# Decoder layer on one core: the last steps of the token-major projections tile by tile, and the output projection's operands in other memory, loaded and split earlier

## The chip, the core and the metric

One Trainium2 chip, one core. The time is that of one execution in device microseconds; the kernel is run several times, and the median is what counts.

## The reference

A decoder layer over 2048 tokens of width 1024, in float32. `_mixer` projects x, sends one part through a gated DeltaNet and the other through a chunked spatial gate, and projects both back; the residual and a layer norm follow. `_hierarchical_moe` then picks two of 64 experts for each token and applies them; a second residual and norm end the layer.

```python
def _mixer(h, w_in, ..., w_out):
    proj = h @ w_in
    qkv, z, b_raw, a_raw, u, v = jnp.split(proj, splits, axis=-1)
    y_dn = _gated_deltanet(qkv, z, b_raw, a_raw, ...)
    y_sgu = _spatial_gating(u, v, ...)
    return jnp.concatenate([y_dn, y_sgu], axis=-1) @ w_out
...
x = _layernorm(ALPHA * x + mixer(x))
x = _layernorm(ALPHA * x + moe(x))
```

## The kernel before

Every large product is made of three matmuls (`mm3`, L135 to L137): each operand is split into a high and a low part, high by ScalarE (`split`, L129), low by VectorE (L130), and high x high, high x low and low x high are summed in PSUM. The splits of one stream of pieces are handled by a `Feed` (from L188): `load` issues the transfers on the SyncE queue, up to two pieces ahead; `split` splits one piece; `get` hands out the oldest.

**Mixer.** Four chunks of 512 tokens, one after the other. Each begins with two token-major projections (`tokmajor`, L381): v and the gates' raw inputs, then v's second part. Four PSUM tiles of 128 tokens (`pz`) run through the eight pieces of the inner dimension (k); then `fin` evacuates the four tiles by the gelu (L439 and L442). Twenty channel-major projections (`chmajor`, tiles `pm`) follow. PSUM has four buffers for all of them, so a projection's first matmul waits until a buffer of the one ahead has been evacuated. Between those matmuls stand the steps of the chunk ahead, as generators that a small scheduler (`Threads`, L71) places: each `yield pe, lat` states how long the step keeps TensorE and how long its result will take, in estimated ns; while the main stream emits its matmuls, the side stream of the highest rank whose time has come is stepped. `attn` and `scan` (L750 to L800) are the DeltaNet's steps: `pa`, then for each of four tiles `pp`, `R`, `pv`, `V`, `pS`, `S`, `p4`, `sq`; `gate_norm` (L503) is the statistics (L509, L510) and the normalisation (L519) of the gelu's result.

**Output projection.** `main_c` works through units of chunk and tiles: three chunks of four tiles, then tiles 0 and 1, tile 2 and tile 3 of the last chunk. A unit has two halves of 512 output columns (z). y^T comes back from memory through a Feed (`yh`, `yl`); the weights `wo`, already split, come through `wload` and `wget`, in pairs of k, two pairs ahead, in a ring of three buffers. In unit KEPT (the third) the weights' ring is closed, and all eight pairs are loaded into a pool of their own (`o_k`), where the last units find them. VectorE evacuates a half with the residual (`xr`, L933). `norm`, `logits` and `route` of a unit run as side streams in the next. The four tiles `po2` use the same four PSUM buffers.

The pools are a stack: what is opened first lies lowest. `o_c` (constants), `o_y` (yh, yl), `o_w` (y^T as loaded), `o_b`, `o_s` and `o_v` (wo) lie over the mixer's pools, so the first use of a place waits for the last reader of what lay there.

**Experts.** 64 experts' weights (`er`) stream through a ring of tiles; the first of its loads are issued in the third unit and behind it (`loads`, L909).

Of the kernel before, what the change touches and what calls it, by code (L numbers as in the profile page):

```python
# [121 lines left out]
class K:  # L122
# [28 lines left out]
    def mixer(self, base, keep, moe_load):  # L151
# [42 lines left out]
        class Feed:  # L194
# [3 lines left out]
            def __init__(f, wp, pieces, parts, depth=2, ahead=2, width=WP):  # L198
# [2 lines left out]
                f.next_load = f.next_split = f.next_get = 0  # L201
                f.limit = len(f.src)

            def load(f):
                while f.next_load < len(f.src) and f.next_load < f.next_split + f.depth:
                    ap, n, width, dst = f.src[f.next_load]
                    r = f.wp.tile([P, f.width], F32, tag="raw", bufs=f.depth, name="wr")
                    rv = r[:, :n * width].rearrange("p (k n) -> p k n", k=n)
                    nc.sync.dma_start(rv, ap)
                    f.raw.append(rv)  # L210
                    f.next_load += 1

            def split(f):
                ap, n, width, dst = f.src[f.next_split]
# [157 lines left out]
        def xsl(t, k, s):  # L372
            return t[k // 2][:, k % 2, s]


        def xpiece(o, q):
            while len(o.xh) <= q:
                h, l = o.feed.get()
                o.xh.append(h), o.xl.append(l)

        def tokmajor(o, width, fin):  # L381

            ps = [psb.tile([P, 512], F32, tag="big", name="pz") for _ in range(TPC)]
            for k in range(KD):
                xpiece(o, k // 2)
                if k % 4 == 0:
                    hi, lo = o.feed.get()
                for t in range(TPC):
                    ts = slice(t * P, (t + 1) * P)
                    self.mm3(ps[t][:, :width], xsl(o.xh, k, ts), xsl(o.xl, k, ts), hi[:, k % 4, :], lo[:, k % 4, :],  # L390
                             k == 0, k == KD - 1)
                    yield 3 * width * 0.42
            for t in range(TPC):
                fin(t, ps[t])

        def chmajor(o, m, fin, last=False):
            if m in PART:
# [455 lines left out]
        scat = []  # L853
        plan = self.plan_consts(keep, cp2)

        def ytile(kp, n):
            return lambda: (yp.tile([P, 2, CH], FR, tag="yh", name="yh").rearrange("p a (b n) -> p (a b) n", n=n),
                            yp.tile([P, 2, CH], FR, tag="yl", name="yl").rearrange("p a (b n) -> p (a b) n", n=n))

        units = [(c, 0, TPC) for c in range(NCH - 1)] + [(NCH - 1, 0, 2), (NCH - 1, 2, 1), (NCH - 1, 3, 1)]
        KEPT = NCH - 2
        pcs = []
        for c, t0, nt in units:
            kp = 1024 // (nt * P)
            pcs += [(self.scr["yT"][c, :, k:k + kp, t0 * P:(t0 + nt) * P], kp, nt * P, ytile(kp, nt * P)) for k in range(0, KD, kp)]
        feed = Feed(wp2, pcs, 0, ahead=0, width=1024)
        wq, kept = [], {}

        def wload():
            if not todo:
                return
            u, z, k = todo.pop(0)
            q = [wpool.tile([P, 2, 512], FR, tag=f"w{j}{'' if u < KEPT else (z, k)}", bufs=3 if u < KEPT else 1, name=f"wo{j}") for j in range(2)]
            for j in range(2):
                nc.sync.dma_start(q[j].bitcast(F32), self.scr["w"][j][:, k:k + 2, z * 512:(z + 1) * 512])
            if u == KEPT:
                kept[z, k] = q
            wq.append(q)  # L880

        todo = [(u, z, k) for u in range(KEPT + 1) for z in range(2) for k in range(0, KD, 2)]

        def wget():
            q = wq.pop(0)
            if todo and (todo[0][0] < KEPT or kept):
                wload()
            return q
# [5 lines left out]
        def main_c(o, side):  # L894
            c, t0, nt = o.unit
            kp = 1024 // (nt * P)
            o.xr, o.ln, o.done, yy = [], 0, 0, []
            o.st = sp2.tile([P, TPC, 2, 6], F32, tag="st", name="st2")

            def residual(t):  # L900
                rows_of.append((o, t))
                if len(rows_of) > NXR:
                    v, z = rows_of[-1 - NXR]
                    run.until(lambda: v.done > z)
                tt = c * TPC + t0 + t
                o.xr.append(bp2.tile([P, D], F32, tag="xr", bufs=NXR, name="xr"))
                nc.sync.dma_start(o.xr[t], I["x"][tt * P:(tt + 1) * P, :])

            for z in range(2):  # L909
                ps = [psb.tile([P, 512], F32, tag="big", name="po2") for _ in range(nt)]  # L910
                for k in range(KD):
                    if z == 0 and k % kp == 0:
                        yy.append(feed.get())
                    if k % 2 == 0:
                        w = kept[z, k] if o.last else wget()
                    if z == 0 and k < min(nt, 2):
                        residual(k)
                    if z == 0 and k >= KD - 2:
                        for t in range(k - KD + 4, nt, 2):
                            residual(t)  # L920
                    for t in range(nt):
                        yh, yl = (v[:, k % kp, t * P:(t + 1) * P] for v in yy[k // kp])
                        self.mm3(ps[t], yh, yl, w[0][:, k % 2, :], w[1][:, k % 2, :], k == 0, k == KD - 1)
                        yield 650
# [6 lines left out]
                zz = slice(z * 512, (z + 1) * 512)  # L931
                for t in range(nt):
                    nc.vector.scalar_tensor_tensor(o.xr[t][:, zz], o.xr[t][:, zz], ALPHA, ps[t], OP.mult, OP.add)  # L933
# [49 lines left out]

        def route(o):
            c, t0, nt = o.unit
            lg = sp2.tile([P, TPC, 72], F32, tag="lg", name="lg")[:, :nt]
            nc.vector.tensor_tensor(lg, o.pl[:, :nt], bc(br.unsqueeze(1), [P, nt, 72]), OP.add)
            yield from self.route(c * TPC + t0, lg, sp2, psd, io64, rec, onesb, lts, eacc, scat)

        prev.sc = run.add(chain(attn(prev), scan(prev)), 0)  # L990
        before = None
        for _ in range(2):
            wload()
        feed.load()
        for _ in range(TPC + 1):
            run.step(prev.sc)
        for u, unit in enumerate(units):
            o = O()
            o.unit, o.before, o.last = unit, before, u > KEPT
            if u == KEPT:  # L1000
                run.finish(prev.sc)
                run.finish(*prev.outs)
                kst.close()
                right.close()
                moe_load()
                wpool = pool(kst, "o_k", 1, "right")
                for _ in range(2):
                    wload()
            run.main(main_c(o, run.add), 4)
            before = o  # L1010
        kst.close()
# [652 lines left out]
```

## Time and profile before

| what | us |
|---|---|
| median of three runs | 2387.25 |
| lowest and highest | 2384.0 and 2391.9 |
| the profiled execution | 2374.18 |
| its span | 2372.4 |
| TensorE busy | 2199.7 (93%) |
| VectorE busy | 1553.4 (65%) |
| ScalarE busy | 1074.5 (45%) |
| GpSimd busy | 535.4 (23%) |

All times of the profile are counted from the span's start. The profiled execution lies 13 us under the median. TensorE's busy time alone does not say where time is lost; for that the waits are read stage by stage: a wait is the idle time of an engine ahead of an instruction, put down to what ended last before it.

### The profile page before, as it was taken

The numbers are of one execution on the slowest core, as the hardware profiler recorded it, in microseconds if no ns is written. First come the engines' busy times: TensorE is split into PE (matmuls) and PEld (weight loads), VectorE is DVE, ScalarE is ACT, GpSimd is POOL, SyncE is SP. The second block draws the span as 40 slices with busy tenths as digits, with TensorE's granted clock in tenths as the row PEclk, the third lists the DMA queues.
The fourth block names the chain that finished last, engine by engine and source line by source line (L and its number), as shares of the span: only waits on it lengthen the run. The fifth ranks groups of instructions, "written<-read, shape, count | busy, mean of one in ns | idle before, by whom it ended". The sixth has DMA issues, their size and how long they took to land.

```text
span 2372.4 us, 32860 instructions
## 1 busy us (share of the span) xinstructions
PE 2199.7 (93%) x11146; PEld 1587.2 (67%) x11146; DVE 1553.4 (65%) x2543; ACT 1074.5 (45%) x1448; POOL 535.4 (23%) x549
## 2 busy tenths in 40 slices
PE   6999999999989989899499999999999999999966
PEld 5877877877787877788374584567457456745732
DVE  4775677677666756557683693577369357836959
ACT  2543254345425422212373583566258356635822
POOL 1113222221222221123521221122122111212115
PEclk8999999999999999999699999999999999999979
DMA  4333234233414356682599999999999999999946
GB/s 150 100 116 112 67 111 120 72 90 102 124 52 126 93 170 227 222 292 98 214 342 407 379 409 408 403 402 399 393 395 388 390 399 371 394 397 385 389 160 285
DMA packets 218898, 601.97 MB, mean 254 GB/s; under 512 B 49632, under 2 KB 70624, under 8 KB 216928
## 3 DMA queue, kind: packets, MB, share of 16 engines
q1 hardware_dynamic: 199840, 563.92, 64.5%
q0 software_dynamic: 18304, 33.77, 3.8%
q8 instruction: 90, 1.47, 0.3%
q10 hardware_dynamic: 576, 2.10, 0.2%
q14 instruction: 88, 0.72, 0.1%
HBM read 557.14 MB, written 65.60 MB: 262 GB/s over the span
## 4 chain that ended last, share of the span: by engine, by line
PE 54%; DMA 24%; DVE 10%; issue 4%; ACT 3%; another core or an unknown queue 2%; POOL 1%; SPq 1%; POOLq 0%; ACTq 0%; DVEq 0%
DMA er<-in_w_e 21%; PE pm L135 5%; PE pm L137 5%; PE pm L136 5%; PE pg L1384 3%; PE pu L1384 3%; PE po L135 2%; PE po L136 2%; PE po L137 2%; DVE elo L130 2%; PE epd L1426 2%; PE epd L1427 2%; PE epd L1429 2%; DMA y<-scr_y 1%
## 5 line engine op out<-in xcount | busy, mean ns | idle before, releaser
L130 DVE TENSOR_TENSOR elo<-er,ehi 128x1024 fp32r<-128x1024 f32 x468 | 549.6, 1219 | 146.8 <-ACT ehi L129 127.6
L129 ACT ACTIVATE ehi<-er 128x1024 fp32r<-128x1024 f32 x468 | 477.9, 1056 | 133.5 <-DMA er<-in_w_e 74.6
L135 PE MATMUL pm<-xh,whi 128*128 128x512 f32 x640 | 270.3, 422 | 5.6 <-ACT vg L442 5.6
L1437 POOL DMA_INDIRECT scr_y<-f,tix x54 | 78.2, 1449 | 865.8 <-DVE f L1436 700.8
L137 PE MATMUL pm<-xh,wlo 128*128 128x512 f32 x640 | 256.3, 400 | 0.0
L136 PE MATMUL pm<-xl,whi 128*128 128x512 f32 x640 | 256.1, 400 | 0.0
L130 DVE TENSOR_TENSOR wlo<-wr,whi 128x1024 fp32r<-128x1024 f32 (+1 forms) x104 | 134.8, 1296 | 70.9 <-ACT whi L129 70.9
L135 PEld LDWEIGHTS pm<-xh,whi 128*128 128x128 f32 x640 | 123.4, 193 | 30.6 <-ACT vg L442 6.1
L137 PEld LDWEIGHTS pm<-xh,wlo 128*128 128x128 f32 x640 | 122.9, 192 | 29.8 <-DVE wlo L130 1.0
L136 PEld LDWEIGHTS pm<-xl,whi 128*128 128x128 f32 x640 | 123.6, 193 | 23.2 <-issue 1.0
L1384 PE MATMUL pg<-er,exT 128*64 128x512 f32 x480 | 136.4, 609 | 1.6 <-DMA er<-in_w_e 1.6
L135 PE MATMUL pg<-ehi,exh 128*128 128x512 f32 x312 | 133.6, 428 | 4.4 <-ACT ehi L129 2.6
L136 PE MATMUL pg<-elo,exh 128*128 128x512 f32 x312 | 127.8, 409 | 8.2 <-DVE elo L130 6.5
L130 DVE TENSOR_TENSOR exl<-ept,exh 128x512 fp32r<-128x512 f32 x78 | 50.2, 683 | 130.0 <-ACT exh L129 129.8
L1384 PE MATMUL pu<-er,exT 128*64 128x512 f32 x480 | 131.1, 593 | 0.0
L129 ACT ACTIVATE whi<-wr 128x1024 fp32r<-128x1024 f32 (+1 forms) x104 | 110.5, 1063 | 43.7 <-DMA wr<-in_w_v 19.3
L1420 PE MATMUL epd<-er,hTw 128*64 128x512 f32 x480 | 125.4, 603 | 2.4 <-DMA er<-in_w_e 2.4
L1426 PE MATMUL epd<-ehi,hT 128*128 128x512 f32 x312 | 126.9, 407 | 0.7 <-ACT hT L129 0.7
L1427 PE MATMUL epd<-elo,hT 128*128 128x512 f32 x312 | 124.6, 399 | 0.5
L135 PE MATMUL po<-wo,yh 128*128 128x512 f32 x256 | 107.0, 418 | 17.8 <-DMA wo<-scr_w 6.9
L137 PE MATMUL pg<-ehi,exl 128*128 128x512 f32 x312 | 123.0, 394 | 0.0
L135 PE MATMUL pu<-ehi,exh 128*128 128x512 f32 x312 | 122.9, 394 | 0.0
(331 smaller groups left out, 4482.6 us busy)
## 6 DMA issues: line engine op xcount, KB each, us to landing
er<-in_w_e SPq DMA_DIRECT2D x768, 512.0 KB
wr<-in_w_q SPq DMA_DIRECT2D x80, 512.0 KB
wo<-scr_w SPq DMA_DIRECT2D x48, 512.0 KB
y<-scr_y SPq DMA_DIRECT2D x14, 1024.0 KB
wr<-in_w_v SPq DMA_DIRECT2D x16, 520.0 KB
wr<-in_xT SPq DMA_DIRECT2D x16, 512.0 KB
wr<-scr_yT SPq DMA_DIRECT2D x16, 512.0 KB
xr<-in_x SPq DMA_DIRECT2D x16, 512.0 KB
```

Source lines behind the costliest of these rows:

```text
L129: nc.scalar.activation(hi, src, AF.Copy)
L130: (engine or nc.vector).tensor_tensor(lo, src, hi.bitcast(F32), OP.subtract)
L135: nc.tensor.matmul(out, xh, wh, start=start, stop=False)
L136: nc.tensor.matmul(out, xh, wl, start=False, stop=False)
L137: nc.tensor.matmul(out, xl, wh, start=False, stop=stop)
L1384: nc.tensor.matmul(ps[r, :], g.xT[:, k, r], g.ws[s][k][:, z * DE:(z + 1) * DE], start=k == 0, stop=k == KD - 1)
L1420: nc.tensor.matmul(pd[r, :], g.hT[:, k, r], g.ws[s][KD + k][:, zz], start=k == 0, stop=k == 3)
L1426: nc.tensor.matmul(pd, g.hT[0][:, k, :], hi_[:, zz], start=k == 0, stop=False)
L1427: nc.tensor.matmul(pd, g.hT[0][:, k, :], lo_[:, zz], start=False, stop=False)
L1429: nc.tensor.matmul(pd, g.hT[1][:, k, :], hi_[:, zz], start=False, stop=k == 3)
L1437: ins = nc.gpsimd.indirect_dma_start(out=self.scr["y"], out_offset=ioff(g.idx[:, 2:3]), in_=g.f, in_offset=None, bounds_check=2 * S - 1, o ...
```

## The change

Six parts. `staggered` goes through all but the last two k for all tiles, and then takes each tile through the last two k by itself; `tokmajor` evacuates a tile where it ends, and so does `main_c`. The pools are opened in another order: `m_b` of the mixer ahead of `m_x` and `m_w`, and `o_b`, `o_s` ahead of `o_y`, `o_w`, `o_v`, so that these last lie where x^T and the projections' weights lay. The first two loads of y^T and of wo, and two splits, stand ahead of the constants. The five steps of `attn` and `scan` that ran ahead of the first unit are gone; `attn`'s last step now states a latency. In unit KEPT the first three pairs of weights go through the old ring, fetched ahead in the unit before, and the other five into `o_k`. In the units from KEPT on an expert load is issued at every other k, and `lg` has two buffers.

```diff
+        bp = pool(left, "m_b", 2, "left")
         xp = pool(left, "m_x", 4, "left")
         wp = pool(left, "m_w", 2, "left")
-        bp = pool(left, "m_b", 2, "left")
...
+        def staggered(nt):
+            for k in range(KD - 2):
+                for t in range(nt):
+                    yield k, t, t == 0, False
+            for t in range(nt):
+                for k in range(KD - 2, KD):
+                    yield k, t, t == 0, k == KD - 1
...
+            for k, t, first, end in staggered(TPC):
+                if first:
+                    xpiece(o, k // 2)
+                    if k % 4 == 0:
+                        hi, lo = o.feed.get()
...
+                if end:
+                    fin(t, ps[t])
+                yield 3 * width * 0.42
...
-                yield 870, 0
+                yield 870, 0 if t < TPC - 1 else 2500
...
         cp2 = pool(base, "o_c", 1, "left")
+        bp2 = pool(base, "o_b", 2, "left")
+        sp2 = pool(base, "o_s", 1, "left")
         yp = pool(base, "o_y", 4, "left")
         wp2 = pool(base, "o_w", 2, "left")
-        bp2 = pool(base, "o_b", 2, "left")
-        sp2 = pool(base, "o_s", 1, "left")
         kst = ExitStack()
-        wpool = pool(kst, "o_v", 1, "left")
+        wpool = [pool(kst, "o_v", 1, "left")]
...
+            if len(kept) < 3:
+                q = [wpool[0].tile([P, 2, 512], FR, tag=f"w{j}", bufs=3, name=f"wo{j}") for j in range(2)]
+            else:
+                q = [wpool[1].tile([P, 2, 512], FR, tag=f"w{j}{z}{k}", bufs=1, name=f"wo{j}") for j in range(2)]
...
+        for _ in range(2):
+            feed.load_one()
+            wload()
+        for _ in range(2):
+            feed.split()
         g1 = cp2.tile([P, D], F32, name="g1")
...
+                    if end:
+                        nc.vector.scalar_tensor_tensor(o.xr[t][:, zz], o.xr[t][:, zz], ALPHA, ps[t], OP.mult, OP.add)
+                    yield 650
+                    if t < nt - 1:
+                        continue
...
-                    if u >= KEPT and len(loads) > RING[1]:
+                    if u >= KEPT and k % 2 and len(loads) > RING[1]:
                         loads.pop(0)()
...
-        for _ in range(2):
-            wload()
-        feed.load()
-        for _ in range(TPC + 1):
-            run.step(prev.sc)
...
-                kst.close()
                 right.close()
                 moe_load()
-                wpool = pool(kst, "o_k", 1, "right")
-                for _ in range(2):
-                    wload()
+                wpool.append(pool(kst, "o_k", 1, "right"))
+                wload()
```

What the scheduler makes of it, at three places. First the SyncE queue (SP) at the end of the second unit and the start of the third; `wr<-scr_yT` are loads of y^T, `wo` the weights, each pair of k being two loads. Before:

```order
190 L877 DMA wo_8642<-scr_w_63 128x2x512
191 L877 DMA wo_8643<-scr_w_64 128x2x512
192 L209 DMA wr<-scr_yT 128x1024
193 L209 DMA wr<-scr_yT 128x4x256 x2
194 L877 DMA wo_8807<-scr_w_63 128x2x512
195 L877 DMA wo_8808<-scr_w_64 128x2x512
196 L877 DMA wo_8811<-scr_w_63 128x2x512
197 L877 DMA wo_8812<-scr_w_64 128x2x512
198 L877 DMA wo_8820<-scr_w_63 128x2x512
199 L877 DMA wo_8821<-scr_w_64 128x2x512
```

Now:

```order
189 L209 DMA wr<-scr_yT 128x1024
190 L868 DMA wo_8702<-scr_w_63 128x2x512
191 L868 DMA wo_8703<-scr_w_64 128x2x512
192 L209 DMA wr<-scr_yT 128x4x256
193 L868 DMA wo_8749<-scr_w_63 128x2x512
194 L868 DMA wo_8750<-scr_w_64 128x2x512
195 L209 DMA wr<-scr_yT 128x4x256
196 L868 DMA wo_8820<-scr_w_63 128x2x512
197 L868 DMA wo_8821<-scr_w_64 128x2x512
198 L868 DMA wo_8829<-scr_w_63 128x2x512
```

Before, all of the third unit's weights stood behind the two y^T loads of 4x256; now two of its pairs (8702 with 8703, 8749 with 8750) stand ahead of the second of them.

VectorE (DVE) at the second border of chunk 1, where the gelu's statistics meet the scan of the chunk ahead (`S`). Before, from the end of the fourth group of statistics:

```order
498 L510 BN_AGGR mv<-st 128x2
499 L512 TENSOR_SCALAR rs<-mv 128x4
500 L519 TENSOR_SCALAR vg<-vg,mv,rs 128x128 x4
501 L130 TENSOR_TENSOR wlo<-wr,whi 128x1024
502 L790 SCALAR_TENSOR_TENSOR S_158<-S_157,eg,pS 128x128 x4
503 L794 TENSOR_TENSOR o<-o,p_4392 128x512
504 L367 TENSOR_REDUCE ro<-sq 128x4
```

Now, from the end of the third group:

```order
483 L524 BN_AGGR mv<-st 128x2
484 L526 TENSOR_SCALAR rs<-mv 128x4
485 L804 SCALAR_TENSOR_TENSOR S_157<-S_158,eg,pS 128x128 x4
486 L808 TENSOR_TENSOR o<-o,p_4295 128x512
487 L371 TENSOR_REDUCE ro<-sq 128x4
488 L812 TENSOR_TENSOR ro<-ro,rq_3505 128x4
489 L813 TENSOR_SCALAR ro<-ro 128x4
490 L523 BN_STATS st<-vg 128x6
```

`S` stood behind four groups, a normalisation and a split; now it stands behind three groups, and the fourth group follows it.

ScalarE (ACT) at the start of the output projection: the first splits `yh` and the scan's `V` and `sq`. Before:

```order
495 L693 ACTIVATE Q_154<-pq 64x2x64 x2
496 L129 ACTIVATE yh<-wr 128x1024
497 L786 ACTIVATE V<-pv 128x512
498 L129 ACTIVATE yh<-wr 128x1024
499 L366 ACTIVATE sq<-o 128x512
500 L786 ACTIVATE V<-pv 128x512
501 L129 ACTIVATE yh<-wr 128x1024
502 L366 ACTIVATE sq<-o 128x512
```

Now:

```order
498 L707 ACTIVATE Q_154<-pq 64x2x64 x2
499 L129 ACTIVATE yh<-wr 128x1024 x2
500 L800 ACTIVATE V<-pv 128x512
501 L370 ACTIVATE sq<-o 128x512
502 L129 ACTIVATE yh<-wr 128x1024
503 L800 ACTIVATE V<-pv 128x512
504 L370 ACTIVATE sq<-o 128x512
505 L129 ACTIVATE yh<-wr 128x1024
506 L800 ACTIVATE V<-pv 128x512
507 L370 ACTIVATE sq<-o 128x512
508 L800 ACTIVATE V<-pv 128x512
```

Two splits stand ahead of the scan's first `V`; the third and the fourth each stand behind a `V` and an `sq`.

## Rows read from the trace of the kernel before

**Rows 1.** Windows of each stage: length, busy time of each engine, granted clock, DMA share, GB/s.

```profile
0.00:837.00 837.00, 777.99 (x4562) 652.42 (x4563) 572.99 (x1178) 354.68 (x591) 190.88 (x256) 0.96 0.34 102
837.00:1124.00 287.00, 262.53 (x1517) 220.92 (x1516) 169.01 (x386) 60.76 (x96) 66.07 (x75) 0.96 0.60 206
1140.00:1164.00 24.00, 1.52 (x9) 0.70 (x9) 15.12 (x80) 0.82 (x4) 13.34 (x20) 0.50 0.25 89
1168.00:2249.00 1081.00, 1065.63 (x4776) 660.04 (x4777) 695.77 (x720) 619.49 (x717) 212.14 (x154) 1.00 1.01 390
```

**Rows 2.** Waits of PE at chunk 1's two borders: us, times, longest.

```profile
PE pp L355 <- DVE S L790: 2.5, 1, 2.5
PE pm L135 <- ACT vg L442: 1.9, 1, 1.9
PE pz L135 <- ACT vg L439: 1.7, 1, 1.7
```

**Rows 3.** Timeline of DVE behind chunk 1's second border: start, length, line, operation.

```profile
255.91 0.29 DVE L509 BATCH_NORM_STATS2 st<-vg 128x6 f32<-128x128 f32 x1
...
257.63 0.17 DVE L512 TENSOR_SCALAR rs<-mv 128x4 f32<-128x4 f32 x1
...
267.26 1.11 DVE L790 SCALAR_TENSOR_TENSOR S<-S,eg,pS 128x128 f32<-128x128 f32 x4
```

**Rows 4.** Waits of PE from 850 to 1070, in the output projection.

```profile
PE po L135 <- DMA wo<-scr_w: 6.9, 1, 6.9
PE po L135 <- ACT yh L129: 4.9, 2, 4.6
PE po L135 <- DVE xr L933: 3.1, 2, 2.4
PE po L135 <- issue: 2.9, 1, 2.9
PE pp L355 <- DVE dec L755: 2.5, 1, 2.5
PE po L136 <- DMA wo<-scr_w: 1.6, 2, 1.3
PE po L137 <- DVE yl L130: 0.9, 2, 0.5
```

**Rows 5.** Windows around four waits: busy time of each engine, granted clock, DMA share.

```profile
251.00:256.00 5.00, 4.57 (x21) 4.30 (x22) 3.64 (x7) 2.15 (x6) 3.01 (x2) 0.66 0.13 29
862.00:870.00 8.00, 6.58 (x19) 5.09 (x20) 1.83 (x2) 1.32 (x2) 0.00 (x0) 0.57 0.55 163
998.00:1008.00 10.00, 5.74 (x17) 4.30 (x18) 9.16 (x29) 4.05 (x4) 2.49 (x2) 0.66 1.03 384
1061.00:1066.00 5.00, 3.40 (x15) 2.83 (x16) 4.93 (x10) 0.00 (x0) 0.00 (x0) 1.00 0.00 0
```

**Rows 6.** Timeline of the SP queue at the output projection's start.

```profile
853.12 11.81 SPq L209 DMA_DIRECT2D wr<-scr_yT  x3
```

**Rows 7.** Timelines of ACT and DVE at the first to the second unit.

```profile
932.22 1.06 ACT L129 ACTIVATE yh<-wr 128x1024 fp32r<-128x1024 f32 x1 [5.04 <-PE po L136]
...
933.31 1.23 DVE L130 TENSOR_TENSOR yl<-wr,yh 128x1024 fp32r<-128x1024 f32 x1 [4.69 <-ACT yh L129]
```

**Rows 8.** Timeline of the SP queue at the second to the third unit.

```profile
984.54 11.60 SPq L209 DMA_DIRECT2D wr<-scr_yT  x3
996.25 3.02 SPq L877 DMA_DIRECT2D wo<-scr_w  x6
```

**Rows 9.** Timelines of DVE and POOL behind the third unit's start.

```profile
995.67 2.47 DVE L933 SCALAR_TENSOR_TENSOR xr<-xr,po 128x512 f32<-128x512 f32 x4
...
1006.53 3.33 POOL L962 TENSOR_TENSOR xr<-xr,b 128x1024 f32<-128x1024 f32 x1 [3.75 <-DVE xr L961]
```

**Rows 10.** Timeline of PE in the second unit, first and last of 27 matmuls.

```profile
945.75 0.40 PE L135 MATMUL po<-wo,yh 128*128 128x512 f32 x1
...
951.84 0.39 PE L137 MATMUL po<-wo,yl 128*128 128x512 f32 x1
```

More of the change, by code (lines that the diff above doesn't have):

```diff
@@ L202, in __init__, with load_one @@
                 f.limit = len(f.src)
+            def load_one(f):
+                ap, n, width, dst = f.src[f.next_load]
+                r = f.wp.tile([P, f.width], F32, tag="raw", bufs=f.depth, name="wr")
+                rv = r[:, :n * width].rearrange("p (k n) -> p k n", k=n)
+                nc.sync.dma_start(rv, ap)
+                f.raw.append(rv)
+                f.next_load += 1
             def load(f):
                 while f.next_load < len(f.src) and f.next_load < f.next_split + f.depth:
[L206 to L211, printed above, removed]
+                    f.load_one()
             def split(f):
@@ L823, in mixer, with ytile, wload, wget @@
         cp2 = pool(base, "o_c", 1, "left")
+        bp2 = pool(base, "o_b", 2, "left")
+        sp2 = pool(base, "o_s", 1, "left")
         yp = pool(base, "o_y", 4, "left")
         wp2 = pool(base, "o_w", 2, "left")
-        bp2 = pool(base, "o_b", 2, "left")
-        sp2 = pool(base, "o_s", 1, "left")
         kst = ExitStack()
-        wpool = pool(kst, "o_v", 1, "left")
+        wpool = [pool(kst, "o_v", 1, "left")]
+        def ytile(kp, n):
+            return lambda: (yp.tile([P, 2, CH], FR, tag="yh", name="yh").rearrange("p a (b n) -> p (a b) n", n=n),
+                            yp.tile([P, 2, CH], FR, tag="yl", name="yl").rearrange("p a (b n) -> p (a b) n", n=n))
+        units = [(c, 0, TPC) for c in range(NCH - 1)] + [(NCH - 1, 0, 2), (NCH - 1, 2, 1), (NCH - 1, 3, 1)]
+        KEPT = NCH - 2
+        pcs = []
+        for c, t0, nt in units:
+            kp = 1024 // (nt * P)
+            pcs += [(self.scr["yT"][c, :, k:k + kp, t0 * P:(t0 + nt) * P], kp, nt * P, ytile(kp, nt * P)) for k in range(0, KD, kp)]
+        feed = Feed(wp2, pcs, 0, ahead=0, width=1024)
+        wq, kept = [], {}
+        def wload():
+            if not todo:
+                return
+            u, z, k = todo.pop(0)
+            if len(kept) < 3:
+                q = [wpool[0].tile([P, 2, 512], FR, tag=f"w{j}", bufs=3, name=f"wo{j}") for j in range(2)]
+            else:
+                q = [wpool[1].tile([P, 2, 512], FR, tag=f"w{j}{z}{k}", bufs=1, name=f"wo{j}") for j in range(2)]
+            for j in range(2):
+                nc.sync.dma_start(q[j].bitcast(F32), self.scr["w"][j][:, k:k + 2, z * 512:(z + 1) * 512])
+            if u == KEPT:
+                kept[z, k] = q
+            wq.append(q)
+        todo = [(u, z, k) for u in range(KEPT + 1) for z in range(2) for k in range(0, KD, 2)]
+        def wget():
+            q = wq.pop(0)
+            wload()
+            return q
+        for _ in range(2):
[3 more added lines that the diff above has]
+            feed.split()
         g1 = cp2.tile([P, D], F32, name="g1")
@@ L854, in mixer @@
         plan = self.plan_consts(keep, cp2)
[L856 to L886, printed above, removed]
-                wload()
-            return q
         NXR, rows_of = 6, []
@@ L910, in main_c @@
                 ps = [psb.tile([P, 512], F32, tag="big", name="po2") for _ in range(nt)]
[L911 to L924, printed above, removed]
+                zz = slice(z * 512, (z + 1) * 512)
+                for k, t, first, end in staggered(nt):
+                    if first:
+                        if z == 0 and k % kp == 0:
+                            yy.append(feed.get())
+                        if k % 2 == 0:
+                            w = kept[z, k] if o.last else wget()
+                        if z == 0 and k < min(nt, 2):
+                            residual(k)
+                        if z == 0 and k >= KD - 2:
+                            for v in range(k - KD + 4, nt, 2):
+                                residual(v)
+                    yh, yl = (v[:, k % kp, t * P:(t + 1) * P] for v in yy[k // kp])
+                    self.mm3(ps[t], yh, yl, w[0][:, k % 2, :], w[1][:, k % 2, :], k == 0, k == KD - 1)
+                    if end:
[3 more added lines that the diff above has]
+                        continue
                     if z == 1 and (k + 1) % kp == 0 and feed.next_split < len(pcs):
                         feed.split()
-                    if u >= KEPT and len(loads) > RING[1]:
+                    if u >= KEPT and k % 2 and len(loads) > RING[1]:
                         loads.pop(0)()
```

21 lines of the change are left out of this document (5 added, 16 removed).

## Prediction

> **What bounds the kernel now.** I read the windows by stage first, then the waits of the matmul engine, then the granted clock around each wait, and last what the transfer queue and the side engines did there. In the mixer's 837 us and the output projection's 287 us TensorE is busy 93% and 91% of the time and the DMA share is 0.34 and 0.60 [rows 1]: there the matmuls and the holes between them set the time. In the expert stage, 1081 us long, TensorE is busy 98.6% and the DMA share is 1.01 [rows 1]; no hole is left in it. The change touches only the first two stages, so all it can win is holes on TensorE, and the reduced clock that follows some of them.
>
> The mixer's holes that the change touches are at the two borders after the token-major projections of chunks 1 to 3. The listed waits stand for chunk 1: 1.7 us for the gelu of the first projection (L439), 1.9 us for that of the second (L442), 2.5 us for S (L790) [rows 2]. Chunks 2 and 3 repeat them within 0.2 us. S is late since DVE stands in one long row of normalisation work: the first BN_STATS of a group starts at 255.91, its rs at 257.63, four such groups stand ahead of S, which runs at 267.26 [rows 3].
>
> In the output projection the waits are 6.9 and 1.6 us for wo, 4.9 for yh, 3.1 for the evacuation of the residual (L933), 2.9 marked issue, 2.5 for dec, 0.9 for yl: 22.8 us [rows 4].
>
> After some of these holes the clock goes from 2.4 to 1.2 GHz for a while. The loss is (1 - granted clock) x window: 0.34 x 5 = 1.7 us at 251, and the mixer has five such stretches among its nine border waits; 0.43 x 8 = 3.4 us at 862, the same again at 934, and 0.34 x 10 = 3.4 us at 998 [rows 5]. Together 8.5 + 10.2 = 18.7 us.
>
> **The change part by part.**
>
> *First border of the mixer.* The last two k are done tile by tile, and each tile is evacuated as it ends. The next projection's first tile needs the first PSUM tile, whose gelu now starts three tiles (18 matmuls) earlier; 1.7 us is covered. Chunks 1 to 3 win 3 x 1.7 = 5.2. Chunk 0's stays: there the scalar engine stands before a split that waits for its load.
>
> *Second border.* 1.9 + 2.5 = 4.4 us go in each chunk, but new ones come. The DVE rows show that S now stands right behind the third group of statistics and that the fourth group lies between it and the R that the next scan step needs. A group takes 1.7 us [rows 3]. Following each matmul to its producer I get about 1.4 us (pp for S), 1.9 (pv for R) and 0.9, in all 4.2. Bounds: nothing, and three groups of 1.7, 5.1. I take 4.2, as the queue is full there. Net 0.2 x 3, nothing.
>
> *Clock in the mixer.* Where a wait of 3.8 to 4.4 is cut into pieces, some of the five stretches should go. I keep three of five: 2 x 1.7 = 3.4 won. Bounds: all gone, 8.5; or four more come, -6.8.
>
> *Start of the output projection.* Before, the first y^T load is issued at 853.12, behind the constants and four weight loads [rows 6], since its tile lay over ones used to the end of the mixer. Now its memory is x^T's and the projection weights', free after the last projection (837), and two splits stand ahead of the constants, so they wait only for the side engines, still busy with the merge of chunk 3. The yh wait (4.9), dec (2.5) and yl (0.9) are 8.3. New: a split is 1.06 us on the scalar engine and 1.23 on DVE [rows 7], and the third and fourth are issued when their k comes; the ACT rows show V and sq of the scan ahead of each. Laying these durations out in the new order I get 1.3 for the first piece, 1.85 for the third, 3.7 for the fourth, whose split stands behind an sq that itself waits for matmuls just ahead. Sum 6.9; bounds nothing and four full splits, 4 x 2.3 = 9.2. Clock: 3.4 now, I leave 1.7. Net 8.3 - 6.9 + 1.7 = 3.1.
>
> *Between the halves of a unit.* The 3.1 us of waits for L933 are two: 2.4, the longest, from the third to the fourth unit, and 0.7 at the border of the first unit's halves [rows 4]. The second goes: 0.7.
>
> *First to second unit.* The 2.9 us stand while yh (932.22), yl (933.31) and four evacuations end one after the other [rows 4, 7]. With the tiles evacuated as they end, nothing is left to wait for: 2.9 and the clock's 3.4, 6.3.
>
> *Second to third unit.* Six weight loads are issued at 996.25, behind three y^T loads that held the queue for 11.6 us from 984.54 [rows 8]; TensorE waits 6.9 and then 1.3 of the 1.6 [rows 4]. By the rows of the queue two pairs of these weights now stand ahead of that held load. 8.2 and the clock's 3.4 go: 11.6. What is late next is the norm: transposes of the first normalised tile stand 60 matmuls behind the border; 26 take 951.84 - 945.75 = 6.09 us, so 60 take 14.1 [rows 10]. From the evacuation to the end of the bias on POOL it is 1006.53 + 3.33 - 995.67 = 14.2 [rows 9], of which three evacuations (1.85) now lie ahead of the border, and the last, behind a split, may come up to 1.2 + 1.8 later. So 12.3 to 15.5 against 14.1: a wait of 0 to 1.4. I take 1.4. Net 10.2.
>
> *Third to fourth unit.* 2.4 + 0.3 go, 1.4 comes for the same reason: 1.3.
>
> *At nothing:* the dropped run-ahead steps (the scan's first steps come among the first matmuls instead; hidden while DVE is free, else in the start's bound); fewer expert loads issued in the third unit (the queue's share in 1140 to 1164 is 0.25 [rows 1]: the ring is full long before the experts start); the second buffer for the logits; the tail after the last matmul, in which the same chain of router, scatters and plan runs.
>
> **The sum.** 5.2 + 0 + 3.4 + 3.1 + 0.7 + 6.3 + 10.2 + 1.3 = 30.2 us. The profiled execution took 2374.2; it would take 2344. That execution lies 13 us under the median of the runs, 2387.25, against which the result is measured: 2387.25 - 30.2 = **2357**. 0.3% of this kernel, about 7 us, is what a measurement can tell from no change.
>
> **The rivals.**
>
> *A, slower.* The change cuts long holes into short ones, and each short one might be followed by a reduced clock. I count nine new waits at the mixer's borders and five in the output projection. If each costs the 3.4 us of rows 5, that is 48 against 18.5 of waits won on balance and 18.7 of old clock loss: 48 - 37 = +10, **2397**; it decides from eleven such drops. Against it: the wait of 2.4 at 1062 left the clock at 1.00 [rows 5], and four of nine border waits did so too. The Trainium skill's page "TensorE: Matmul & The Clock Gate", section "A second HAM failure mode: psum-queue depth-cycling", speaks for it: a kernel that cycles PSUM banks with frequent short idling there lost throughput to the clock falling and rising between bursts. By that rule the time would be 2397; the trace so far bears it out at five of nine waits, and not at 1062. Chance 0.05.
>
> *B, half.* The splits and the normalisation come just in time: the start wins nothing (-3.1), the mixer's clock stays as it is (-3.4), one clock loss of 3.4 remains at a unit border, and the weights fetched ahead arrive 5 late since the held load still blocks the third pair. 30.2 - 14.9 = 15: **2372**. For it: DVE is the late engine in both places. Chance 0.20.
>
> *C, more.* The new waits are covered and no reduced clock is left: 18.5 + 18.7 = 37, **2350**, and with half of the 12 us of new waits hidden, 2344. For it: every new wait is shorter than the hole it replaces. Chance 0.18.
>
> *D, nothing.* The expert weights' stream sets the end, and an earlier start only waits for it. For it: its DMA share is 1.01 [rows 1]. Against: from 1140 to 1164 that share is 0.25, the ring stands full and waits for the first experts to free it, so the stream starts with them, and moves with them. 2387, chance 0.07.
>
> **How the numbers follow.** Forecast 0.50, A 0.05, B 0.20, C 0.18, D 0.07. Of the forecast's own range the bounds are the start (0 to 9.2 for 6.9), the second border (0 to 15 for 12.6) and the clock (8.5 to -6.8 for 3.4): about 10 to each side, 2347 to 2367. With B and C and some scatter of the runs the range is 2341 to 2374; A, D and the ends of B and C are left out. Faster: 0.50 + 0.20 + 0.18 = 0.88; same 0.07; slower 0.05.
>
> **What would show it.** In the profile after: of the four waits of pz for the first gelu only chunk 0's left; pp and pv waits of 1 to 2 us at the second border; yh and yl waits summing to about 7 us at the start, the worst at the fourth piece; no wait for wo between the second and third unit, but one of pt up to 1.4; the granted clock at 1.00 at the first unit border. Experts starting about 30 us earlier with the same length. Wrong if the expert stage grows, if wo is still waited for, or if the windows of the mixer show more than five reduced stretches at the borders.

## The result and the profile after

| kernel | runs | median us (lowest to highest) | ratio to before | 95% interval |
|---|---|---|---|---|
| before | 4 | 2385.62 (2375.60 to 2391.90) | 1 | |
| the change | 4 | 2348.55 (2342.11 to 2350.69) | 0.985 | 0.9816 to 0.9883 |

The change is 1.5% faster. It was forecast at 2357, in a range of 2341 to 2374; by the medians it wins 37 us where the sum said 30.2. The two profiled executions lie 23.5 us apart: that of before (2374.18) was shorter than its four runs in the table, that of the change (2350.69) is the longest of its four. So a part of the 37 is in no profile; a later section follows that.

The windows by stage, as in [rows 1] (the second from the last `pm` to the last `po`). The mixer is 6 us shorter, the output projection 19 (287 to 268), its granted clock went from 0.96 to 0.99, and 1081 us of the expert stage are as full as before, on TensorE and on the DMA. The first matmul of the experts starts at 1145.1 instead of 1167.9, and 1204 us follow it in both. Before it, in the third window, the queue stands as idle as it did: the stream of expert weights moved with its start.

```profile
0.00:831.00 831.00, 778.85 (x4564) 653.06 (x4564) 570.56 (x1178) 356.69 (x591) 189.55 (x256) 0.95 0.34 103
830.70:1098.50 267.80, 256.31 (x1516) 218.41 (x1515) 169.86 (x381) 61.03 (x96) 68.30 (x75) 0.99 0.63 218
1115.00:1140.00 25.00, 1.51 (x9) 0.69 (x9) 15.38 (x82) 0.82 (x4) 14.52 (x22) 0.50 0.22 79
1145.00:2226.00 1081.00, 1064.87 (x4777) 659.89 (x4778) 696.41 (x720) 619.98 (x718) 211.64 (x154) 1.00 1.01 390
```

The waits at chunk 1's borders, which answer to [rows 2]: those for the two gelus are gone, pp waits 3.1 for S, and pv 1.9 in two for R.

```profile
PE pp L359 <- DVE S L804: 3.1, 1, 3.1
PE pv L359 <- DVE R L792: 1.9, 2, 1.2
```

VectorE there, as in [rows 3]: three groups of statistics from 245.19 to 250.50, then S, then the fourth group up to 255.70 and R behind it.

```profile
245.19 0.28 DVE L523 BATCH_NORM_STATS2 st<-vg 128x6 f32<-128x128 f32 x1
...
250.50 0.17 DVE L526 TENSOR_SCALAR rs<-mv 128x4 f32<-128x4 f32 x1
250.58 1.12 DVE L804 SCALAR_TENSOR_TENSOR S<-S,eg,pS 128x128 f32<-128x128 f32 x4
...
255.70 0.17 DVE L526 TENSOR_SCALAR rs<-mv 128x4 f32<-128x4 f32 x1
255.78 0.68 DVE L791 TENSOR_TENSOR R<-pp,eg 128x512 f32<-128x512 f32 x1
```

The waits in the output projection, as in [rows 4]. Of 22.8 us 10 are left, and none of any size is for wo.

```profile
PE po L137 <- DVE yl L130: 3.6, 3, 2.4
PE po L135 <- ACT yh L129: 2.9, 2, 2.5
PE pt L365 <- POOL xr L985: 1.9, 2, 1.0
PE po L135 <- DVE xr L947: 1.3, 1, 1.3
...
PE po L136 <- DMA wo<-scr_w: 0.2, 1, 0.2
```

The clock around some of those places, as in [rows 5]: 0.66 behind the wait for S, 0.66 at the start of the output projection and 0.67 behind its longest wait, 1.00 at the first to the second (922) and the second to the third unit (977). The last row is a merge of DeltaNet steps with the projections, ahead of the border of chunk 3.

```profile
251.00:256.00 5.00, 5.00 (x25) 4.68 (x26) 4.06 (x17) 0.63 (x1) 1.81 (x3) 0.66 0.00 0
845.00:850.00 5.00, 4.39 (x20) 3.87 (x21) 3.67 (x7) 0.84 (x1) 3.89 (x11) 0.66 0.39 118
882.00:887.00 5.00, 4.41 (x21) 3.94 (x22) 2.48 (x3) 0.00 (x0) 2.93 (x2) 0.67 0.47 131
922.00:927.00 5.00, 5.00 (x24) 4.14 (x23) 4.07 (x8) 1.07 (x1) 0.00 (x0) 1.00 0.91 290
977.00:982.00 5.00, 5.00 (x24) 4.12 (x23) 3.96 (x11) 1.06 (x1) 0.00 (x0) 1.00 0.74 237
610.00:632.00 22.00, 21.59 (x126) 17.43 (x127) 10.40 (x22) 5.78 (x15) 3.69 (x4) 0.53 0.31 100
```

The same place in the kernel before:

```profile
619.00:632.00 13.00, 12.34 (x94) 9.54 (x94) 8.47 (x17) 6.04 (x15) 3.27 (x4) 0.74 0.48 159
```

There lies the mixer's missing gain in this pair of profiles. The reduced clock cost 0.26 x 13 = 3.4 us there before, and 0.47 x 22 = 10.3 in this execution, though the order of the instructions in that merge is nearly the same.

The windows also part the waits from the clock. Over the mixer and the output projection TensorE's idle time (length less busy time) fell from 59.0 + 24.5 to 52.2 + 11.5 us, by 19.8; its busy time fell by 5.4. In the output projection alone these are 13.0 and 6.2. Busy time stands for the clock here, since it grows at the lower one: in the kernel before a matmul of 512 columns starts every 0.43 us at 1004, at 1.2 GHz, and every 0.23 us at 1007.

The SyncE queue at the start, which answers to [rows 6]: the first piece of y^T is asked for at 821.47, 10 us ahead of the mixer's end and 32 us earlier than before; the second follows at 831.84, both ahead of the constants. The third waits until 846.26, for the first split.

```profile
821.47 0.32 SPq L209 DMA_DIRECT2D wr<-scr_yT  x1
...
831.84 0.46 SPq L209 DMA_DIRECT2D wr<-scr_yT  x1
...
846.26 2.54 SPq L209 DMA_DIRECT2D wr<-scr_yT  x2
848.85 0.42 SPq L886 DMA_DIRECT2D g<-in_ln_g  x1
```

ScalarE at the fourth split, which answers to [rows 7]: it starts only when sq is done, which waited 6.1 us for VectorE.

```profile
880.21 0.63 ACT L370 ACTIVATE sq<-o 128x512 f32<-128x512 f32 x1 [6.11 <-DVE o L808]
880.75 1.04 ACT L129 ACTIVATE yh<-wr 128x1024 fp32r<-128x1024 f32 x1
```

The queue at the second to the third unit, as in [rows 8]: two pairs of weights go out at 969.18 and 974.66, before the load that was held (now from 980.65).

```profile
969.18 0.88 SPq L868 DMA_DIRECT2D wo<-scr_w  x2
...
974.66 1.65 SPq L868 DMA_DIRECT2D wo<-scr_w  x2
980.65 0.36 SPq L209 DMA_DIRECT2D wr<-scr_yT  x1
981.11 2.06 SPq L868 DMA_DIRECT2D wo<-scr_w  x4
```

### The profile page after: what moved, and what is told of

It reads as the page before. It is cut to its first block, busy times and chain, and to the rows that moved or that the text cites. A ratio compares the mean times of both kernels' runs of the same rounds, so it can differ in the third digit from the quotient of the medians.

```text
span 2348.9 us, 32846 instructions
## 1 busy us (share of the span) xinstructions
PE 2193.9 (93%) x11146; PEld 1585.1 (67%) x11146; DVE 1553.6 (66%) x2543; ACT 1077.0 (46%) x1448; POOL 536.1 (23%) x549
## 4 chain that ended last, share of the span: by engine, by line
PE 52%; DMA 25%; DVE 11%; issue 4%; ACT 3%; another core or an unknown queue 2%; POOL 2%; SPq 0%; DVEq 0%; POOLq 0%; ACTq 0%
DMA er<-in_w_e 22%; PE pm L135 5%; PE pm L137 5%; PE pm L136 5%; PE pg L1400 3%; PE pu L1400 2%; PE po L137 2%; PE po L135 2%; PE po L136 2%; DVE elo L130 2%; PE epd L1442 2%; PE pz L135 1%; PE epd L1443 1%; PE epd L1445 1%
## 5 line engine op out<-in xcount | busy, mean ns | idle before, releaser
L137 PE MATMUL pu<-ehi,exl 128*128 128x512 f32 x312 | 122.3, 392 | 0.0
```

The lines of the kernel that those rows point to most:

```text
L137: nc.tensor.matmul(out, xl, wh, start=False, stop=stop)
```

## The experiments

All were timed against the kernel before in the same series; the kernels of a series share its runs. The medians of the kernel before were 2383.14 (first four), 2378.94 (next four) and 2381.59 us (last).

| kernel | median us | ratio to before | 95% interval |
|---|---|---|---|
| no_stagger_proj | 2356.54 | 0.9880 | 0.9838 to 0.9922 |
| no_early_start | 2348.70 | 0.9849 | 0.9807 to 0.9890 |
| no_fetch_ahead | 2359.97 | 0.9887 | 0.9845 to 0.9929 |
| no_stagger_out | 2357.51 | 0.9897 | 0.9853 to 0.9941 |
| change_again | 2350.18 | 0.9855 | 0.9809 to 0.9901 |
| stats_apart | 2344.09 | 0.9834 | 0.9786 to 0.9883 |
| split_earlier | 2345.78 | 0.9841 | 0.9796 to 0.9886 |
| both_apart | 2337.83 | 0.9810 | 0.9764 to 0.9855 |
| both_further | 2332.44 | 0.9785 | 0.9754 to 0.9816 |
| both_and_logits | 2331.76 | 0.9792 | 0.9762 to 0.9821 |

The intervals are 0.3 to 0.5% to each side, 7 to 12 us, as wide as single terms; the first four kernels were not timed beside the change. So each part is also read in the trace, as the length of its own stage. The output projection, from the last `pm` to the last `po`, took 286.9 us before (836.8 to 1123.7) and 267.8 after.

**The projections as before (no_stagger_proj).**

```diff
-            for k, t, first, end in staggered(TPC):
+            for k in range(KD):
+                for t in range(TPC):
...
+            for t in range(TPC):
+                fin(t, ps[t])
```

> The change with the mixer's token-major projections as before (all tiles through all k, then four evacuations); the rest as in the change. By the prediction's terms (5.2 us of waits at the first border, 3.4 us of clock) this is 8.6 us slower than the change, about 2357 us. Rival: the new waits for S and R at the second border give back what the first border won, and the clock falls as often; then it is within 3 us of the change. In its profile the 1.7 us waits for the first gelu are back in chunks 1 to 3, and the pv waits for R at the second border are gone.

Measured: 8 us over the change's first median. Its waits at chunk 1's borders:

```profile
PE pp L359 <- DVE S L804: 3.1, 1, 3.1
PE pv L359 <- DVE R L792: 2.2, 2, 1.2
PE pz L135 <- ACT vg L453: 1.6, 1, 1.6
```

The first gelu's wait is back, as forecast (5.4 us in four over the mixer). But pp and pv still wait as in the change: the forecast that these go was wrong. Nor do the wait for the second gelu and the two reduced stretches come back: three are left at these borders, as in the change. So 5.2 of the forecast 8.6 is shown; that the median moved by 8 does not show the 3.4 us of clock. The wait for S does not come from the staggering; the order in which the scheduler places S and the statistics came with the change's other edits. In no_early_start below, which has the old latency of `attn` and the old pools, it is another again: pp waits 11.3 us in three, pv 2.9 in three, where the change has 9.3 in three and 5.8 in six. The latency and the pools were not tried apart, and neither were the expert loads at every other k and the second buffer of `lg`.

**The start as before (no_early_start).** The old order of the pools, no early loads and splits, the five steps ahead restored, and the old latency of `attn`'s last step; the cut shows the loads and the steps.

```diff
-        for _ in range(2):
-            feed.load_one()
-            wload()
-        for _ in range(2):
-            feed.split()
...
+        for _ in range(2):
+            wload()
+        feed.load()
+        for _ in range(TPC + 1):
+            run.step(prev.sc)
```

> The change with the output projection's start as before: the old order of the pools, the constants ahead of the first loads of y^T, no early splits, five steps of attn and scan run ahead. The prediction's term is 3.1 us: about 2352 us. Rival: the profile after has the first matmul of the output projection 18 us earlier, 12 of it gained between the last projection and that matmul, and loses some 6 again in the first unit, so 6 us or more: 2355 us or above.

Measured: no difference in the median. Its output projection:

```profile
844.60:1114.90 270.30, 257.95 (x1515) 217.21 (x1514) 168.16 (x381) 61.14 (x96) 66.48 (x75) 0.99 0.63 218
```

270.3 us, 2.5 more than the change's 267.8. Counted from the end of the last projection, the first matmul starts after 13.8 us in the change and after 26.3 here, but most of these 12 us is given back at once, in waits for yl and yh of 2.4, 2.5 and 0.6 us and in steps of the scan that no longer stand ahead of it. 2.5 us is what is left in one profile of each, near the 3.1 forecast; the medians are too coarse to show it, and the rival's 6 is not borne out.

**The third unit's weights as before (no_fetch_ahead).**

```diff
-            if len(kept) < 3:
+            if u < KEPT:
...
+                kst.close()
                 right.close()
                 moe_load()
                 wpool.append(pool(kst, "o_k", 1, "right"))
-                wload()
+                for _ in range(2):
+                    wload()
```

> The change with the third unit's weights as before: the ring closed ahead of it, all eight pairs loaded into their own pool behind the border. The prediction's term is 10.2 us: about 2359 us, with the wait of 7 to 8 us for wo back at the third unit. Rival: with the tiles evacuated as they end, something else holds the border (the held y^T load, the norm), and it is 5 us or less: 2354 us or below.

Measured: 11 us over the change's median. Output projection 278.4 us, 10.6 over the change's:

```profile
850.40:1128.80 278.40, 259.44 (x1516) 220.01 (x1514) 169.97 (x381) 61.13 (x96) 68.38 (x75) 0.97 0.61 210
```

```profile
PE po L135 <- DVE eacc L1187: 8.0, 1, 8.0
PE po L136 <- DMA wo<-scr_w: 2.2, 2, 1.3
```

The wait of 8 us is back. The profile names eacc of VectorE for it; the weights are issued at 1002.00 in this execution, behind a load of y^T, and the matmul starts at 1006.84 and goes on waiting for wo. Of the 10.6 us 7.5 are idle time of TensorE and 3.1 busy time, where the forecast had 6.8 of waits and 3.4 of clock. The forecast's 10.2 is confirmed; the rival is out.

**The output projection's tiles as before (no_stagger_out).**

```diff
-                for k, t, first, end in staggered(nt):
+                for k, t, first in [(k, t, t == 0) for k in range(KD) for t in range(nt)]:
...
-                    if end:
-                        nc.vector.scalar_tensor_tensor(o.xr[t][:, zz], o.xr[t][:, zz], ALPHA, ps[t], OP.mult, OP.add)
...
+                for t in range(nt):
+                    nc.vector.scalar_tensor_tensor(o.xr[t][:, zz], o.xr[t][:, zz], ALPHA, ps[t], OP.mult, OP.add)
```

> The change with the output projection's tiles as before (all tiles through all k, then the evacuations); the rest as in the change. The prediction's terms are 0.7, 6.3 and 1.3 us, 8.3 in all: about 2357 us, with a wait of about 3 us and a reduced clock at the border of the first to the second unit. Rival: the clock's loss there came from that execution alone; then 4 us or less.

Measured: 9 us over the change's median; in the trace its output projection is 273.0 us, 5.2 over the change's.

```profile
924.00:930.00 6.00, 3.18 (x15) 2.48 (x14) 4.82 (x8) 1.06 (x1) 0.00 (x0) 1.00 0.86 281
982.00:988.00 6.00, 3.68 (x10) 2.94 (x11) 5.54 (x10) 0.36 (x1) 0.00 (x0) 0.72 0.97 319
832.20:1105.20 273.00, 257.26 (x1516) 219.82 (x1515) 171.00 (x386) 60.80 (x96) 67.93 (x75) 0.98 0.62 214
```

```profile
PE po L135 <- issue: 5.2, 2, 2.8
PE po L135 <- DVE xr L956: 2.4, 1, 2.4
```

The waits at the unit borders are back (2.8 and 2.4 marked issue, 2.4 for xr), but the clock was 1.00 after the first of them and fell only at the second: 0.28 x 6 = 1.7 lost, not 3.4. The trace says 5.2, the prediction 8.3; TensorE's idle time is 4.2 longer than in the change (4.9 forecast), so most of the difference is the clock. That is the rival's reason, though its 4 us or less did not come.

The three stage lengths add up: 2.5 + 10.6 + 5.2 = 18.3 of the 19.1 us by which the output projection became shorter. That leaves 0.8 for the parts that were not tried.

**The change once more (change_again).**

> The change itself, beside the kernels it is to be compared with. If the 37 us of the first comparison were waits and reduced clock of every execution, 2345 to 2352 us and 33 to 38 us under the kernel before. If the 17 us that the waits do not explain were chance of four runs, the difference is nearer 25 to 30. In every run the span times the mean granted clock should be about 18 to 20 us less than before's 2290.

Measured: 2350.18, within the first alternative's times, but 29 us under the median of before in that series, which is the second's; the ratio, 0.9855, is the first one's. So a part of the 37 us may be the chance of few runs. The output projection is again 268.0 us, with 11.9 us of idle time. The mixer, though, took 839.2 us in this execution, 2 more than in the first profile of before. The merge ahead of chunk 3 lost 0.39 x 35 = 13.7 us here:

```profile
838.80:1106.80 268.00, 256.07 (x1515) 218.47 (x1514) 169.84 (x381) 61.17 (x96) 68.33 (x75) 0.99 0.63 218
610.00:645.00 35.00, 33.27 (x208) 26.23 (x208) 15.28 (x31) 11.51 (x28) 7.51 (x8) 0.61 0.38 121
```

Each run lists its span and its mean granted clock; their product takes the time lost at the lower clock off the span. It takes off too much, since a stretch at the lower clock counts even where TensorE is idle. For the kernel before it is 2285 to 2293 in all eleven runs of this series, while the spans go from 2367 to 2397: most of the spread of the runs is the clock's. The mean product is 2288.7 before and 2270.3 for the change: 18.4 us less, where the terms without clock make 18.3 (30.2 less 11.9; the prediction's 18.5 is a slip). Of the mean times (2382.5 and 2349.6, 33 us apart) that leaves 14.6 to the clock, where the prediction had 11.9.

That the products agree to a tenth is luck in part. For no_stagger_proj, no_early_start, no_fetch_ahead and no_stagger_out they lie 14.7, 18.7, 16.1 and 17.5 us under before's, so by them these parts are worth 3.7, nothing, 2.3 and 0.9 us, 7 in all and not the 18 that their terms make without clock. A wait that falls into a reduced stretch counts half in the product: in no_fetch_ahead 5.1 of the 10.2 us of the stretch at the third unit are idle. The split into waits and clock is therefore an estimate; what the single parts are worth is read from the stages.

**Two more profiles of the kernel before (before_look_1 and before_look_2).**

> The kernel before, for a second profile. Span times granted clock of all its runs is 2285 to 2293, so its spread of 30 us is the clock's. Theory (the merge of the DeltaNet, with its wait of 1.7 us and many small matmuls, is where the reduced stretches differ from run to run): its borders and the output projection lose as in the first profile (five stretches of 3.4 us, three of 6.8), and the stretches near 190, 405 and 620 are 6.8 to 30 us long. Rival: the stretches at the borders or in the output projection are the ones that grow.

> The same kernel once more, the same expectation: a third profile of it.

Measured: 2373.98 and 2371.12 us. Both executions were again among the shortest of the kernel, so neither shows where the others lose up to 25 us. The stretches at the mixer's borders lose as much as in the first profile. The output projection again took 285.3 and 286.2 us, with 25.0 and 25.5 us of idle time (24.5 in the first). But its clock differs: behind the wait of 2.9 us at 934 it was 1.00 in both, where the first profile lost 3.4 us, and the stretch at 998 was 10.2 us long instead of 6.8. The merge from 185 to 206 had a granted clock of 0.67 in before_look_1 and of 0.84 in the first profile. That fits the theory without proving it. Which executions of the kernel before lose more, and where, stays open.

**The statistics apart (stats_apart).**

```diff
                 o.mv.append(mv), o.rs.append(rs)
-                yield 0, 500
+                yield 0, 2500
```

> The change with the stated latency of a group of the gelu's statistics at 2500 instead of 500, so that S and R of the scan stand behind one group each and not behind three. Theory (the waits of pp and pv at the second border, 3.1 + 0.8 + 1.2 us in each of three chunks, are VectorE's queue): 10 to 15 us of waits go and up to three reduced stretches of 1.7, 12 to 18 us under the change. Rival (VectorE is short of time there whatever the order): the waits move to the normalisation and the gain is under 5 us.

Measured: 6 us under change_again. The wait for S is gone and that for R grew to 3.6 at chunk 1:

```profile
PE pv L359 <- DVE R L792: 3.6, 2, 2.2
```

```profile
252.03 1.12 DVE L804 SCALAR_TENSOR_TENSOR S<-S,eg,pS 128x128 f32<-128x128 f32 x4
...
257.16 0.17 DVE L526 TENSOR_SCALAR rs<-mv 128x4 f32<-128x4 f32 x1
257.24 0.68 DVE L791 TENSOR_TENSOR R<-pp,eg 128x512 f32<-128x512 f32 x1
```

S now starts at 252.03, right behind the first group, but the second group ends at 257.16 and R stands behind it. The theory was right on the cause, but its 12 to 18 us did not come: in chunks 1 to 3 the change has 15.1 us of waits for S and R, and 10.9, all for R, are left here.

**The third and fourth split earlier (split_earlier).**

```diff
-        feed = Feed(wp2, pcs, 0, ahead=0, width=1024)
+        feed = Feed(wp2, pcs, 0, ahead=1, width=1024)
+        feed.limit = KD // 2
```

> The change with the third and the fourth split of y^T's first chunk issued one piece earlier. Theory (the yl and yh waits of 2.4, 2.5 and 0.6 us in the first unit come from the place of the splits): they go, 3 to 5 us and one or two reduced stretches of 1.7 us, 4 to 8 us under the change. Rival: the splits then stand ahead of the scan's V and sq, and the scan's matmuls wait instead; within 3 us of the change.

Measured: 4.4 us under change_again; its output projection took 260.5 us, 7.3 less than the change's.

```profile
838.30:1098.80 260.50, 253.80 (x1515) 216.78 (x1514) 169.53 (x381) 61.18 (x96) 67.56 (x75) 0.99 0.65 224
```

```profile
PE po L137 <- DVE yl L130: 0.6, 1, 0.6
PE po L135 <- ACT yh L129: 0.4, 1, 0.4
```

The waits for yl and yh went from 6.5 to 1.0, and the scan did not wait in their place. So the start's term was limited by where two splits stand in ScalarE's row, as the prediction read it from the order.

**Both edits (both_apart).**

> Both edits together. If they are independent, the sum: 16 to 25 us under the change, near 2326 us. If the clock falls at other places instead, half of it.

Measured: 12.4 us under change_again, about the sum of what the two gave alone (6.1 and 4.4) and less than the 16 to 25 forecast for it, which still had the full 12 to 18 of stats_apart in it.

**A group behind R (both_further).** As both_apart, the latency 4000 instead of 2500.

> Both edits, with the latency of a group of statistics at 4000, so that a group stands behind R and not between S and R. Theory: stats_apart won 6 instead of 12 to 18 us since its group of 1.7 us came between S and R, and pv waited for R instead (10.8 us in six waits); with the group behind R those go to some 3 us: 6 to 10 us under both_apart, near 2330 us. Rival: VectorE has no room there, and R or the normalisation is as late: within 3 us of both_apart.

Measured: 5.4 us under both_apart and 18 under change_again by the medians, which come from two series; against the kernel before of its own series it is 49 us faster, both_apart 41. At chunk 1 pv waits 0.5, once, and the clock there is 1.00. The waits for R fell from 10.8 to 1.4 us in all.

```profile
PE pv L359 <- DVE R L792: 0.5, 1, 0.5
```

```profile
245.00:262.00 17.00, 16.54 (x107) 14.51 (x106) 14.77 (x48) 3.59 (x6) 5.16 (x5) 1.00 0.24 69
```

VectorE is busy 14.8 of those 17 us: it has room for the statistics, but only where nothing that TensorE waits for stands behind them. This kernel has a lower median than both_apart, with intervals that overlap.

**The transposes later (both_and_logits).** As both_further, and `side(logits(o), 2, 15500)` instead of 13000.

> As both_further, and the transposes of the normed tile placed 12 matmuls later. Theory (they wait 1.0 and 0.9 us for the bias on POOL, as the prediction's term for the norm said): 2 us under both_further. Rival: the four transposes then come closer together and the residual's buffers free later; no gain, or 1 to 3 us lost.

Measured: no difference (2331.76 against 2332.44); the rival was right. The wait of pt for the bias is gone, and that for the evacuation has grown from 1.7 us to 4.7:

```profile
PE po L135 <- DVE xr L948: 4.7, 2, 4.2
```

## Why the prediction was right

*The method.* The time lies in the range, and most of the mechanism is in the traces: in the output projection TensorE's idle time fell by 13.0 us, where the terms without clock make 13.1, and three profiles of before (24.5, 25.0, 25.5) and two of the change (11.5, 11.9) agree on it. Over both stages idle time fell by 19.8 in the first pair of profiles, against 18.3; the clock gave back 5.4 there, against 11.9. That the runs gained 30.2 and more all the same is partly luck: in the means the clock's share is estimated at 14.6, and which executions had it no profile shows.

*First border.* Right: the waits for the first gelu went in chunks 1 to 3, 5.2 us, and with the projections as before they are back. Chunk 0's stayed, as I held: it was 0.5 in the first profile after, but 2.2 in change_again, where before had 2.5.

*Second border.* Right in kind: S behind three groups, R behind the fourth. The new waits are 3.1 + 0.8 + 1.2 = 5.0 us in each chunk, against 4.2 in the prediction and a bound of 5.1. Over the three chunks the waits at the second border were 13.4 us before and are 15.1 after (16.7 in change_again): 1.7 or 3.3 lost, where I had nothing. The new waits came from the order of the scheduler and not from the cut of the old ones, for they stay without the staggering.

*The mixer's clock.* "I keep three of five": three stretches are left at these borders, one behind each wait for S. But I had looked at the borders alone. Over the whole mixer the first profile after has as much time at the lower clock as before, 75 us. The stretches that differ most between profiles lie in the merges, and there they cost the change more than the borders won. In the merge ahead of chunk 3 the three profiles of before have 6.8 us at the lower clock each; the change has 20.5 and 27.3, and of the nine other kernels, each with most of the change, seven have 20.5 to 30.7 (stats_apart has 6.8, no_stagger_out none). Whether the change brings that on, no run here shows. The mixer as a whole took 837.2, 840.4 and 836.9 us in the profiles of before and 831.1 and 839.2 in those of the change, so its 8.6 us are not shown by them.

*Start.* Sum of the new waits 6.9 forecast, 6.5 measured (0.4 and 0.6 for the first piece, 2.4 for the third, 2.5 and 0.6 for the fourth); two reduced stretches, 0.34 x 5 = 1.7 each, where one was left in the sum. The term is 2.5 in the stage's length against 3.1.

*Unit borders.* The first to the second unit: no wait, clock 1.00, the 6.3 went. With the old loop only 2.8 of it and no clock came back there, and in the two later profiles of before the clock there was 1.00 as well, so the 3.4 of clock was that execution's and not the wait's. Second to third: 10.6 against 10.2, though the 3.4 of clock in it counted some time twice: 3.0 of the 6.8 us at the lower clock were the wait itself. The wait of the transposes that was to take 1.4 takes 1.0 and, a unit later, 0.9. What I had not seen: in the third unit's second half a matmul waits 1.3 us for an evacuation, and that for the residual's load, which the SyncE queue held for 5.6 us until a store of the unit before (`scr_h`) was done:

```profile
1014.42 0.69 DVE L947 SCALAR_TENSOR_TENSOR xr<-xr,po 128x512 f32<-128x512 f32 x1 [5.13 <-DMA xr<-in_x]
```

*The rivals.* A needed eleven reduced stretches of 3.4 us behind the new waits; five came (three at the borders, two at the start), at 1.7 each. The section "A second HAM failure mode: psum-queue depth-cycling" of the Trainium skill's page "TensorE: Matmul & The Clock Gate" has a kernel whose frequent short idling makes the clock fall and rise. The trace agrees at these five and not at the others, the wait of 2.4 us for the start's third piece among them. B had the start winning nothing and the weights late: the queue's rows show the pairs out in time. D is out: the expert stage has kept its length and moved. C's 2350 is nearest to the median, but not by its reason: the new waits were there, in full, and reduced clock was left. In the two series with the change itself the medians are 37 and 29 us apart, so a forecast of 30 and a C of 37 can't be told apart by them.

## What to carry to other kernels

Evacuating a tile when it ends, and asking for the next operands before a held transfer instead of behind it, took away the waits that the trace named, at nearly the prices it gave. What a reduced clock cost behind a wait in one profile is no such price: it may be absent in the next profile of the same kernel. What came in their place was short work on a side engine standing ahead of what TensorE waits for: look at the row of each engine, and move such work behind, not just apart. Where runs scatter by more than a term is worth, take the length of the term's own stage from the trace, and part it into idle and busy time; span times granted clock is an estimate for the whole.

## What was not expected of the hardware

Most of the scatter of the runs is the clock's: the kernel before goes from 2368 to 2400 us at a mean granted clock of 0.967 to 0.954, while the product of span and clock stays between 2285 and 2298. In the merges, where many small matmuls follow a wait of 1.7 us, the time at 1.2 GHz differs most: the merge ahead of chunk 3 lost 3.4 us to it in each of three profiles of before, 10.3 and 13.7 in two of the change. What decides between them no run here shows.
